# Strided attention: another order of the first loads, and keys and values prepared piecemeal

## The chip, the cores and the metric

The kernel runs on one core of a Trainium2 chip. The metric is device time in microseconds, the median of several executions. The core has five engines that work side by side, each through its own list of instructions in order: TensorE (matrix products; PE in the profile, its weight loads PEld), VectorE (DVE), ScalarE (ACT), GpSimd (POOL) and SyncE (SP). Sixteen DMA engines move data between the chip's main memory (HBM) and the on-chip memory. Here all transfers are issued by SyncE, on one queue.

## What is computed

For each of 8 x 12 = 96 heads, 1024 queries of 64 numbers attend to only 16 keys and values: those at the positions 0, 64, 128 and so on. All is float32 on the outside.

```python
batch, heads, seq, dim = (8, 12, 1024, 64)      # stride = 64
scale = 1.0 / np.sqrt(dim)
for i in range(seq):
    attend_positions = np.arange(0, seq, stride)
    q = Q[:, :, i:i + 1, :].copy()
    k = K[:, :, attend_positions, :].copy()
    v = V[:, :, attend_positions, :].copy()
    scores = np.einsum('bhqd,bhkd->bhqk', q, k) * scale
    weights = np.exp(scores - np.max(scores, axis=-1, keepdims=True))
    weights = weights / (np.sum(weights, axis=-1, keepdims=True) + 1e-10)
    result[:, :, i, :] = np.einsum('bhqk,bhkd->bhqd', weights, v)[:, :, 0, :]
```

Q and the result are 25.2 MB each. Of K and V only a sixteenth is read, 0.39 MB each, in rows of 256 bytes that lie 16 KB apart.

## The kernel before

The heads are worked off in 24 groups of four (`HG`, `NG`). A group's Q block is 1 MB and so is its part of the result. `load(g)` (line 94) brings a Q block as 32 rows of 32 KB into one of 11 buffers (`QBUFS`), `store(g)` (line 250) writes a result block from one of 9 (`OBUFS`). Both go through `_copy`, so line 34 is the issue of every such transfer. K and V are loaded by lines 89 and 90.

The order of all work is written out by hand (`manual_schedule`); each engine executes its instructions in the order of the program.

**Start-up.** SyncE issues K, V and then the first 11 Q blocks. GpSimd makes an identity matrix and from it the two orders of rows and columns `perm_k` and `perm_v` (lines 113 and 120), and casts K twice side by side into `k_dup` (line 116) and V into `v_bf` (line 124), both in bfloat16. VectorE clears `k_t` and the three weight buffers `w` (lines 127, 131) and makes a selector of head slots, `s_sel` and `mask` (lines 138 to 151). Then, for all 24 groups at once, TensorE transposes the keys (line 160), ScalarE copies them into `k_t` (line 166), TensorE sorts the values (line 175), and VectorE multiplies them by the mask, four times for each of four matmul results (line 180), which makes the block-diagonal values `v_bd`.

**A group** goes through four functions:

- `transposes(g, x)`, x = 0 and 1: eight TensorE transposes (line 193) take half a Q block, of which they read the upper 16 bits of each float32 number as bfloat16; a ScalarE copy (line 198) brings the result from the accumulators' memory (PSUM) into `qt`, which has two buffers.
- `scores(g)`: four matmuls of `k_t` with `qt` (line 206), then two exponentials on ScalarE (line 218) into the weight buffer `w`.
- `sums(g)`: eight small matmuls of `w` with `s_sel` (line 227), and a reciprocal on VectorE (line 231).
- `outputs(g, c)`, c = 0 to 3: two matmuls of `w` with `v_bd` (line 238), and one VectorE multiplication by the reciprocals (line 243) into the result block.

Ahead of the loop stand the transposes of groups 0 and 1 and the scores of group 0. An iteration of the loop then is: sums of g, outputs 0 and 1, scores of g+1, output 2, the first transposes of g+2, output 3, the second transposes of g+2, the store of g, and the load of g+11.

Of the kernel before, what the change touches and what calls it, by code (L numbers as in the profile page):

```python
# [11 lines left out]
FP32 = mybir.dt.float32  # L12
BF16 = mybir.dt.bfloat16
I16 = mybir.dt.int16
AF = mybir.ActivationFunctionType
ALU = mybir.AluOpType


def _ap_with(ap: bass.AP, new_ap, extra_offset: int = 0) -> bass.AP:
    return dataclasses.replace(  # L20
        ap, ap=[list(p) for p in new_ap], offset=ap.offset + extra_offset
    )
# [26 lines left out]
def kernel(  # L49
# [8 lines left out]
    nc = tc.nc  # L58

    B, H, S, D = Q.shape  # L60
# [3 lines left out]
    P = 128  # L64
    HG = 4
    NG = B * H // HG
    NC = NG // 2
    SD = S * D
    assert B * H == NG * HG and S == 1024 and D == 64 and NK == 16
    QBUFS = 11  # L70
    OBUFS = 9

    const = ctx.enter_context(tc.tile_pool(name="const", bufs=1))
    qn_pool = ctx.enter_context(tc.tile_pool(name="qn", bufs=QBUFS))
    out_pool = ctx.enter_context(tc.tile_pool(name="outsb", bufs=OBUFS))
    qt_pool = ctx.enter_context(tc.tile_pool(name="qt", bufs=2))
    rec_pool = ctx.enter_context(tc.tile_pool(name="rec", bufs=2))
    psum_qt = ctx.enter_context(tc.tile_pool(name="pqt", bufs=2, space=bass.MemoryType.PSUM))
    psum_sc = ctx.enter_context(tc.tile_pool(name="psc", bufs=2, space=bass.MemoryType.PSUM))
# [6 lines left out]
    k_raw = const.tile([P, NC, D], FP32, name="k_raw")  # L86
    v_raw = const.tile([P, NC, D], FP32, name="v_raw")
    kv_src = [[stride * D, P], [2 * HG * SD, NC], [1, D]]
    nc.sync.dma_start(k_raw, _ap_with(K, kv_src))
    nc.sync.dma_start(v_raw, _ap_with(V, kv_src))  # L90

    qn = {}

    def load(g):
        qn[g] = qn_pool.tile([P, 32 * D], FP32, name="qn", tag="qn")
        _copy(
            nc, qn[g], _ap_with(Q, [[HG * SD // 32, 32], [1, HG * SD // 32]], g * HG * SD)
        )

    for g in range(QBUFS):  # L100
        load(g)


# [4 lines left out]
    perm_k = const.tile([P, 2, 2, 2, NK], BF16, name="perm_k")  # L108

    perm_v = const.tile([P, 2, 2, 2, 2, NK], BF16, name="perm_v")  # L110
    for c in range(2):
        for a in range(2):
            nc.gpsimd.tensor_copy(out=perm_k[:, c, a], in_=id_v[:, c, :, a])
    k_dup = const.tile([P, NC, 2, D], BF16, name="k_dup")
    for e in range(2):
        nc.gpsimd.tensor_copy(out=k_dup[:, :, e], in_=k_raw)  # L116
    for c in range(2):
        for a in range(2):
            for e in range(2):
                nc.gpsimd.tensor_copy(  # L120
                    out=perm_v[:, c, a, :, e], in_=id_v[:, c, :, a]
                )
    v_bf = const.tile([P, NC, D], BF16, name="v_bf")
    nc.gpsimd.tensor_copy(out=v_bf, in_=v_raw)  # L124

    k_t = const.tile([P, NC, 2, 4, 2, NK], BF16, name="k_t")
    nc.vector.memset(k_t, 0.0)  # L127
# [1 line left out]
    for i in range(3):  # L129
        w = const.tile([P, 8, P], BF16, name=f"w{i}")  # L130
        nc.vector.memset(w, 0.0)
        w_bufs.append(w)


    iota_p = const.tile([P, 1], I16, name="iota_p")
    nc.gpsimd.iota(iota_p, pattern=[[0, 1]], base=0, channel_multiplier=1)  # L136
    slot_i = const.tile([P, 1], I16, name="slot_i")
    nc.vector.tensor_scalar(  # L138
        out=slot_i, in0=iota_p, scalar1=4, scalar2=3,
# [1 line left out]
    )  # L141
    slot_f = const.tile([P, 1], FP32, name="slot_f")
    nc.vector.tensor_copy(out=slot_f, in_=slot_i)
    col4 = const.tile([P, 4], I16, name="col4")
    nc.gpsimd.iota(col4, pattern=[[1, 4]], base=0, channel_multiplier=0)
    s_sel = const.tile([P, 4], BF16, name="s_sel")
    nc.vector.tensor_scalar(
        out=s_sel, in0=col4, scalar1=slot_f, scalar2=None, op0=ALU.is_equal
    )
    mask = const.tile([P, 4], FP32, name="mask")  # L150
    nc.vector.tensor_scalar(
        out=mask, in0=col4, scalar1=slot_f, scalar2=None, op0=ALU.is_equal
    )


    pk = perm_k.rearrange("p c a b k -> p (c a b k)")
    for n in range(NC // 4):
        kp = psum_o.tile([P, 4, 2, 4, NK], FP32, name="kp", tag="o")
        for i in range(4):
            nc.tensor.matmul(  # L160
                kp[:, i], lhsT=k_dup[:, 4 * n + i].rearrange("p e d -> p (e d)"),
                rhs=pk, start=True, stop=True,
            )
        for e in range(2):
            h = slice(64 * e, 64 * e + 64)
            nc.scalar.copy(  # L166
                k_t[h, 4 * n : 4 * n + 4, :, :, e].rearrange("p n c s k -> p (n c s) k"),
                kp[h].rearrange("p n c s k -> p (n c s) k"),
            )

    v_bd = const.tile([P, NC, 2, 4, D], BF16, name="v_bd")
    for n in range(2):
        for c in range(2):
            vp = psum_sc.tile([P, NC // 2, D], FP32, name="vp", tag="sc")
            nc.tensor.matmul(  # L175
                vp, lhsT=perm_v[:, c].rearrange("p a b e k -> p (a b e k)"),
                rhs=v_bf[:, 6 * n : 6 * n + 6], start=True, stop=True,
            )
            for s in range(4):
                nc.vector.tensor_scalar(  # L180
                    out=v_bd[:, 6 * n : 6 * n + 6, c, s], in0=vp,
                    scalar1=mask[:, s : s + 1], scalar2=None, op0=ALU.mult,
                )

    qt, wt, rec, out_sb = {}, {}, {}, {}

    def transposes(g, x):
        if x == 0:
            qt[g] = qt_pool.tile([P, 2, 8, P], BF16, name="qt", tag="qt")
        ps = psum_qt.tile([P, 8, P], BF16, name="qt_ps", tag="qt_ps")  # L190
        qb = qn[g].bitcast(BF16)
        for i in range(8):
            nc.tensor.transpose(  # L193
                ps[:, i],
                _ap_with(qb, [qb.ap[0], [2, P]], extra_offset=(8 * x + i) * 2 * P + 1),
                identity,
            )
        nc.scalar.copy(qt[g][:, x], ps)  # L198

    def scores(g):  # L200
        sc = psum_sc.tile([P, 512], FP32, name="sc", tag="sc")
        q = qt[g]
        kt = k_t[:, g // 2, g % 2].rearrange("p s e k -> p (s e k)")
        for j in range(4):
            a, b = divmod(j, 2)
            nc.tensor.matmul(  # L206
                sc[32 * j : 32 * j + 32],
                lhsT=kt[:, 32 * j : 32 * j + 32],
                rhs=_ap_with(
                    q, [q.ap[0], [P, 8], [8 * P, 2], [1, 32]],  # L210
                    extra_offset=32 * (2 * b + a),
                ),
                start=True, stop=True, tile_position=(0, 32 * j),
            )
        w = wt[g] = w_bufs[g % 3]
        for a in range(2):
            wa = w[64 * a : 64 * a + 64]
            nc.scalar.activation(  # L218
                out=_ap_with(wa, [wa.ap[0], [P, 8], [1, 2], [2, 32]], extra_offset=64 * a),
                in_=sc[64 * a : 64 * a + 64].rearrange("p (t x q) -> p t x q", t=8, x=2),  # L220
                func=AF.Exp, bias=0.0, scale=scale,
            )

    def sums(g):
        sm = psum_s.tile([P, 2, 8, 2], FP32, name="sm", tag="sm")
        for i in range(8):
            nc.tensor.matmul(  # L227
                sm[:, :, i], lhsT=wt[g][:, i], rhs=s_sel, start=True, stop=True
            )
        rec[g] = rec_pool.tile([P, 2, 16], FP32, name="rec", tag="rec")  # L230
        nc.vector.reciprocal(rec[g], sm.rearrange("p b i e -> p b (i e)"))  # L231

    def outputs(g, c):
        if c == 0:
            out_sb[g] = out_pool.tile([P, 2, 16, D], FP32, name="out_sb", tag="out_sb")
        ps = psum_o.tile([P, 2, 2, 2 * D], FP32, name="o_ps", tag="o")
        for i in range(2):
            nc.tensor.matmul(  # L238
                ps[:, :, i], lhsT=wt[g][:, 2 * c + i],
                rhs=v_bd[:, g // 2, g % 2].rearrange("p s d -> p (s d)"),  # L240
                start=True, stop=True,
            )
        nc.vector.tensor_tensor(  # L243
            out=out_sb[g][:, :, 4 * c : 4 * c + 4],
            in0=ps.rearrange("p b i (e d) -> p b (i e) d", e=2),
            in1=rec[g][:, :, 4 * c : 4 * c + 4].unsqueeze(3).to_broadcast([P, 2, 4, D]),
            op=ALU.mult,
        )

    def store(g):  # L250
        o = out_sb[g]
        _copy(
            nc,
            _ap_with(out, [[16 * D, P], [2 * SD, 2], [1, 16 * D]], g * HG * SD),
            _ap_with(o, [o.ap[0], [1, 1], [1, 32 * D]]),
        )

    for g in range(2):
        for x in range(2):
            transposes(g, x)  # L260
    scores(0)
    for g in range(NG):
        sums(g)
        outputs(g, 0)
        outputs(g, 1)
        if g + 1 < NG:
            scores(g + 1)
        outputs(g, 2)
        if g + 2 < NG:
            transposes(g + 2, 0)  # L270
        outputs(g, 3)
        if g + 2 < NG:
            transposes(g + 2, 1)
        store(g)
        if g + QBUFS < NG:
            load(g + QBUFS)
# [35 lines left out]
```

The softmax here doesn't subtract the row's maximum and nothing guards it: scores larger than these inputs give would overflow.

## Time and profile before

| What | Value | Where it is from |
|---|---|---|
| median of five executions | 130.43 us (130.31 to 130.78) | the times |
| the profiled execution | 130.44 us | the times |
| its span, first to last instruction | 128.6 us | the page |
| busy: PE, PEld, DVE, ACT, POOL | 69.5, 51.3, 83.8, 86.2, 5.1 us | the page |
| moved by DMA | 51.26 MB, mean 399 GB/s | the page |
| one result multiplication, line 243 | 689 ns, 96 times | groups of the page |
| one copy of transposes, line 198 | 1015 ns, 48 times | groups of the page |
| one exponential, line 218 | 736 ns, 48 times | groups of the page |
| one masking of values, line 180 | 609 ns, 16 times | groups of the page |
| one key copy, line 166 | 580 ns, 6 times | groups of the page |
| one cast of K for all groups, line 116 | 829 ns, twice | groups of the page |
| load of a Q block, issue to landing | 18.9 us, median of 24 | DMA issues of the page |
| store of a result block, issue to landing | 19.5 us, median of 24 | DMA issues of the page |

The span counts from the first to the last instruction; the execution's own time has 1.84 us more around it. The page names busy time by engine, a row of forty slices that says how many of the sixteen DMA engines were busy in each, the DMA queues, the chain of work that ended last, and the costliest groups of instructions. Behind the page stand finer views of the same execution: instructions in order of time, waits by who ended them, and sums over chosen stretches. A transfer's time from issue to landing holds its wait in the queue.

### The profile page before, as it was taken

The numbers are of one execution on the slowest core, as the hardware profiler recorded it, in microseconds if no ns is written. First come the engines' busy times: TensorE is split into PE (matmuls) and PEld (weight loads), VectorE is DVE, ScalarE is ACT, GpSimd is POOL, SyncE is SP. The second block draws the span as 40 slices with busy tenths as digits, with TensorE's granted clock in tenths as the row PEclk, the third lists the DMA queues.
The fourth block names the chain that finished last, engine by engine and source line by source line (L and its number), as shares of the span: only waits on it lengthen the run. The fifth ranks groups of instructions, "written<-read, shape, count | busy, mean of one in ns | idle before, by whom it ended". The sixth has DMA issues, their size and how long they took to land.

```text
span 128.6 us, 2215 instructions
## 1 busy us (share of the span) xinstructions
PE 69.5 (54%) x880; PEld 51.3 (40%) x880; DVE 83.8 (65%) x144; ACT 86.2 (67%) x103; POOL 5.1 (4%) x23
## 2 busy tenths in 40 slices
PE   0071665985656866667766668666677666500000
PEld 0040542764445654445544456544455444300000
DVE  6229963788678777787777787777877777740000
ACT  2173294988889888899888898888998888400000
POOL 4470000000000000000000000000000000000000
PEclk9999997799999999999999999999999999955555
DMA  2998989999799899999999999999998999999970
GB/s 62 346 438 377 469 347 489 408 403 469 321 428 489 357 426 446 405 441 436 398 451 433 392 449 441 392 466 428 395 482 349 426 423 426 418 431 421 426 326 18
DMA packets 7722, 51.26 MB, mean 399 GB/s; under 512 B 3872, under 2 KB 3872, under 8 KB 3872
## 3 DMA queue, kind: packets, MB, share of 16 engines
q1 hardware_dynamic: 7712, 51.12, 96.3%
q8 instruction: 7, 0.11, 0.4%
q14 instruction: 3, 0.02, 0.0%
HBM read 25.95 MB, written 25.17 MB: 398 GB/s over the span
## 4 chain that ended last, share of the span: by engine, by line
ACT 59%; PE 14%; DVE 5%; DMA 3%; POOL 3%; issue 3%; ACTq 1%; DVEq 0%; POOLq 0%
ACT qt L198 33%; ACT w L218 26%; PE sc L206 8%; DVE v_bd L180 3%; DMA k_raw<-in_K_dram 3%; PE qt_ps L193 3%; PE o_ps L238 2%; DVE out_sb L243 1%; POOL k_dup L116 1%; POOL perm_v L120 1%; PE sm L227 1%; POOL v_bf L124 1%; ACTq L307 1%; DVEq L307 0%; PE vp L175 0%
## 5 line engine op out<-in xcount | busy, mean ns | idle before, releaser
L243 DVE TENSOR_TENSOR out_sb<-o_ps,rec 128x512 f32<-128x512 f32 x96 | 63.3, 689 | 15.2 <-PE o_ps L238 12.9
L198 ACT COPY qt<-qt_ps 128x1024 bf16<-128x1024 bf16 x48 | 46.2, 1015 | 5.2 <-PE qt_ps L193 4.7
L218 ACT ACTIVATE w<-sc 64x512 bf16<-64x512 f32 x48 | 35.3, 736 | 13.2 <-PE sc L206 12.9
L238 PE MATMUL o_ps<-v_bd,w 128*128 128x256 bf16 x192 | 33.5, 279 | 0.6 <-DVE out_sb L243 0.6
L193 PE MATMUL qt_ps<-identity,qn 128*128 128x128 bf16 x384 | 30.9, 227 | 0.2 <-ACT qt L198 0.2
L193 PEld LDWEIGHTS <-qn 128*128 128x128 bf16 x384 | 27.1, 103 | 3.9 <-issue 2.6
L206 PE MATMUL sc<-qt,k_t 128*32 128x512 bf16 x96 | 9.8, 396 | 24.4 <-ACT qt L198 24.4
L238 PEld LDWEIGHTS <-w 128*128 128x128 bf16 x192 | 14.3, 98 | 6.9 <-issue 6.2
L206 PEld LDWEIGHTS <-k_t 128*32 128x32 bf16 x96 | 4.4, 93 | 29.2 <-issue 29.1
L231 DVE RECIPROCAL rec<-sm 128x32 f32<-128x32 f32 x24 | 8.6, 358 | 8.9 <-PE sm L227 8.9
L227 PE MATMUL sm<-s_sel,w 128*128 128x4 bf16 x192 | 8.5, 166 | 6.8 <-ACT w L218 4.8
L227 PEld LDWEIGHTS <-w 128*128 128x128 bf16 x192 | 6.4, 96 | 10.9 <-ACT w L218 10.9
L180 DVE TENSOR_SCALAR v_bd<-vp,mask 128x384 bf16<-128x384 f32 x16 | 8.5, 609 | 0.1
L166 ACT CAST k_t<-kp 64x512 bf16<-64x512 f32 x6 | 3.5, 580 | 3.5 <-PE kp L160 3.4
L160 PE MATMUL kp<-perm_k,k_dup 128*128 128x128 bf16 x12 | 1.5, 309 | 6.6 <-POOL k_dup L116 6.6
L175 PE MATMUL vp<-v_bf,perm_v 128*128 128x384 bf16 x4 | 1.8, 490 | 4.6 <-DVE v_bd L180 4.1
L160 PEld LDWEIGHTS <-k_dup 128*128 128x128 bf16 x12 | 1.2, 141 | 6.6 <-POOL k_dup L116 6.6
L138 DVE TENSOR_SCALAR slot_i<-iota_p 128x1 int16<-128x1 int16 x1 | 0.2, 156 | 4.6 <-POOL iota_p L136 4.6
L166 ACT ACT_TABLE_LOAD x1 | 1.3, 1283 | 2.5 <-DVE k_t L127 2.5
L127 DVE MEMSET k_t<- 128x1536 uint32 x1 | 1.3, 1338 | 1.1 <-PEq L293 1.1
L175 PEld LDWEIGHTS <-perm_v 128*128 128x128 bf16 x4 | 0.5, 126 | 3.7 <-issue 3.7
L116 POOL CAST k_dup<-k_raw 128x768 bf16<-128x768 f32 x2 | 1.6, 829 | 2.9 <-DMA k_raw<-in_K_dram 2.9
(15 smaller groups left out, 6.0 us busy)
## 6 DMA issues: line engine op xcount, KB each, us to landing
qn<-in_Q_dram SPq DMA_DIRECT2D x24, 1024.0 KB, 18.9
out_dram<-out_sb SPq DMA_DIRECT2D x24, 1024.0 KB, 19.5
k_raw<-in_K_dram SPq DMA_DIRECT2D x1, 384.0 KB, 4.2
v_raw<-in_V_dram SPq DMA_DIRECT2D x1, 384.0 KB, 5.4
```

Source lines behind the costliest of these rows:

```text
L116: nc.gpsimd.tensor_copy(out=k_dup[:, :, e], in_=k_raw)
L160: nc.tensor.matmul(kp[:, i], lhsT=k_dup[:, 4 * n + i].rearrange("p e d -> p (e d)"), rhs=pk, start=True, stop=True,)
L166: nc.scalar.copy(k_t[h, 4 * n : 4 * n + 4, :, :, e].rearrange("p n c s k -> p (n c s) k"), kp[h].rearrange("p n c s k -> p (n c s) k"),)
L180: nc.vector.tensor_scalar(out=v_bd[:, 6 * n : 6 * n + 6, c, s], in0=vp, scalar1=mask[:, s : s + 1], scalar2=None, op0=ALU.mult,)
L193: nc.tensor.transpose(ps[:, i], _ap_with(qb, [qb.ap[0], [2, P]], extra_offset=(8 * x + i) * 2 * P + 1), identity,)
L198: nc.scalar.copy(qt[g][:, x], ps)
L206: nc.tensor.matmul(sc[32 * j : 32 * j + 32], lhsT=kt[:, 32 * j : 32 * j + 32], rhs=_ap_with(q, [q.ap[0], [P, 8], [8 * P, 2], [1, 32]], ext ...
L218: nc.scalar.activation(out=_ap_with(wa, [wa.ap[0], [P, 8], [1, 2], [2, 32]], extra_offset=64 * a), in_=sc[64 * a : 64 * a + 64].rearrange( ...
L227: nc.tensor.matmul(sm[:, :, i], lhsT=wt[g][:, i], rhs=s_sel, start=True, stop=True)
L231: nc.vector.reciprocal(rec[g], sm.rearrange("p b i e -> p b (i e)"))
L238: nc.tensor.matmul(ps[:, :, i], lhsT=wt[g][:, 2 * c + i], rhs=v_bd[:, g // 2, g % 2].rearrange("p s d -> p (s d)"), start=True, stop=True,)
L243: nc.vector.tensor_tensor(out=out_sb[g][:, :, 4 * c : 4 * c + 4], in0=ps.rearrange("p b i (e d) -> p b (i e) d", e=2), in1=rec[g][:, :, 4 ...
```

## The change

- Q block 0 is loaded first, then K and V, then Q blocks 1 to 10. Later loads and stores keep their order.
- Keys are prepared in three parts of eight groups. `keys(n)` casts a third of K on VectorE instead of GpSimd, transposes it and copies it. The first part stands ahead of the loop, the others at the end of iterations 1 and 3.
- V is cast on VectorE. The sorted values are copied unmasked into `v_rep` by `value_rows()`, in four copies; `values(g)` then multiplies them by a mask for one group at a time on GpSimd, into one of three buffers `vb`, two groups ahead in the loop. `outputs` reads `vb[g]` instead of `v_bd`.
- The mask is now 128 x 4 x 64 bfloat16 numbers, and the two small index tables are made earlier.
- The start-up order is: transposes of group 0, first keys, scores of group 0, values, transposes of group 1. An iteration is: values and the first transposes of g+2, sums of g, output 0, scores of g+1, output 1, second transposes of g+2, outputs 2 and 3, in iterations 1 and 3 a third of the keys, the store of g, the load of g+11.

```diff
+    vb_pool = ctx.enter_context(tc.tile_pool(name="vb", bufs=3))
...
-    nc.sync.dma_start(k_raw, _ap_with(K, kv_src))
-    nc.sync.dma_start(v_raw, _ap_with(V, kv_src))
...
-    for g in range(QBUFS):
+    load(0)
+    nc.sync.dma_start(k_raw, _ap_with(K, kv_src))
+    nc.sync.dma_start(v_raw, _ap_with(V, kv_src))
+    for g in range(1, QBUFS):
         load(g)
...
-    k_dup = const.tile([P, NC, 2, D], BF16, name="k_dup")
-    for e in range(2):
-        nc.gpsimd.tensor_copy(out=k_dup[:, :, e], in_=k_raw)
...
-    v_bf = const.tile([P, NC, D], BF16, name="v_bf")
-    nc.gpsimd.tensor_copy(out=v_bf, in_=v_raw)
...
-    mask = const.tile([P, 4], FP32, name="mask")
-    nc.vector.tensor_scalar(
-        out=mask, in0=col4, scalar1=slot_f, scalar2=None, op0=ALU.is_equal
-    )
...
+    mask = const.tile([P, 4, D], BF16, name="mask")
+    nc.vector.tensor_copy(out=mask, in_=s_sel.unsqueeze(2).to_broadcast([P, 4, D]))
...
+    def keys(n):
+        for e in range(2):
+            nc.vector.tensor_copy(
+                out=k_dup[:, 4 * n : 4 * n + 4, e], in_=k_raw[:, 4 * n : 4 * n + 4]
+            )
         kp = psum_o.tile([P, 4, 2, 4, NK], FP32, name="kp", tag="o")
...
-            for s in range(4):
-                nc.vector.tensor_scalar(
-                    out=v_bd[:, 6 * n : 6 * n + 6, c, s], in0=vp,
-                    scalar1=mask[:, s : s + 1], scalar2=None, op0=ALU.mult,
...
+    def value_rows():
+        nc.vector.tensor_copy(out=v_bf, in_=v_raw)
+        for n in range(2):
+            for c in range(2):
+                vp = psum_sc.tile([P, NC // 2, D], FP32, name="vp", tag="sc")
+                nc.tensor.matmul(
+                    vp, lhsT=perm_v[:, c].rearrange("p a b e k -> p (a b e k)"),
+                    rhs=v_bf[:, 6 * n : 6 * n + 6], start=True, stop=True,
                 )
+                nc.vector.tensor_copy(out=v_rep[:, 6 * n : 6 * n + 6, c], in_=vp)
...
+    def values(g):
+        vb[g] = vb_pool.tile([P, 4, D], BF16, name="vb", tag="vb")
+        nc.gpsimd.tensor_tensor(
+            out=vb[g], in0=mask,
+            in1=v_rep[:, g // 2, g % 2].unsqueeze(1).to_broadcast([P, 4, D]),
+            op=ALU.mult,
+        )
...
-                rhs=v_bd[:, g // 2, g % 2].rearrange("p s d -> p (s d)"),
+                rhs=vb[g].rearrange("p s d -> p (s d)"),
...
-    for g in range(2):
-        for x in range(2):
-            transposes(g, x)
+    transposes(0, 0)
+    transposes(0, 1)
+    keys(0)
     scores(0)
+    value_rows()
+    values(0)
+    values(1)
+    transposes(1, 0)
+    transposes(1, 1)
     for g in range(NG):
+        if g + 2 < NG:
+            values(g + 2)
+            transposes(g + 2, 0)
         sums(g)
         outputs(g, 0)
-        outputs(g, 1)
         if g + 1 < NG:
             scores(g + 1)
-        outputs(g, 2)
-        if g + 2 < NG:
-            transposes(g + 2, 0)
-        outputs(g, 3)
+        outputs(g, 1)
         if g + 2 < NG:
             transposes(g + 2, 1)
+        outputs(g, 2)
+        outputs(g, 3)
+        if g in (1, 3):
+            keys((g + 1) // 2)
         store(g)
```

## The prediction

> **What bounds the kernel now.** The page comes first: the span, the DMA row, the queues, and the chain that ended last.
>
> ```profile
> span 128.6 us, 2215 instructions
> ...
> DMA  2998989999799899999999999999998999999970
> ...
> q1 hardware_dynamic: 7712, 51.12, 96.3%
> q8 instruction: 7, 0.11, 0.4%
> ...
> ACT 59%; PE 14%; DVE 5%; DMA 3%; POOL 3%; issue 3%; ACTq 1%; DVEq 0%; POOLq 0%
> ```
>
> Two readings compete. The chain is 59% ScalarE, so it looks as if the transpose copies (L198) and exponentials (L218) set the time. The queue row says that packets of SyncE's own queue fill 96.3% of what 16 DMA engines have in the whole span. What decides is the end: who waits for whom on SyncE, and when it issues.
>
> ```profile
> SPq L307 <- DMA out_dram<-out_sb: 12.8, 1, 12.8
> ```
>
> ```profile
> 0.74 0.44 SPq L89 DMA_DIRECT2D k_raw<-in_K_dram  x1
> 1.23 0.71 SPq L90 DMA_DIRECT2D v_raw<-in_V_dram  x1
> 1.99 12.61 SPq L34 DMA_DIRECT2D qn<-in_Q_dram  x11
> 25.15 0.63 SPq L34 DMA_DIRECT2D out_dram<-out_sb  x1
> ...
> 60.08 0.47 SPq L34 DMA_DIRECT2D qn<-in_Q_dram  x1
> ...
> 64.98 0.47 SPq L34 DMA_DIRECT2D qn<-in_Q_dram  x1
> ...
> 82.16 32.50 SPq L34 DMA_DIRECT2D out_dram<-out_sb  x11
> ```
>
> The last store is issued at 82.16 + 32.50 = 114.7 us, when all arithmetic is over, and SyncE then waits 12.8 us for stores already in the queue. One group moves one load and one store and takes 64.98 - 60.08 = 4.90 us there, while the ScalarE part of the chain repeats every 3.94 us (its exponentials start at 38.43 and 42.37). So compute runs ahead and stands in line behind the DMA engines. The chain view doesn't see this, since it follows the instructions and not the packets. Only three things can move the end: bytes, time in which DMA engines stand idle, and the rate of packets. The stretches with DMA engines below 1.00 are at the two ends (columns: stretch, length, busy time of PE, PEld, DVE, ACT, POOL, clock, share of 16 DMA engines, GB/s; a share over 1 means small packets that overlap in one engine):
>
> ```profile
> 0.00:1.83 1.83, 0.00 (x0) 0.00 (x0) 0.70 (x1) 0.00 (x0) 1.17 (x10) 1.00 0.00 0
> 1.83:2.23 0.40, 0.00 (x0) 0.00 (x0) 0.40 (x1) 0.00 (x0) 0.20 (x2) 1.00 0.29 74
> 2.23:2.63 0.40, 0.00 (x0) 0.00 (x0) 0.34 (x2) 0.08 (x1) 0.00 (x0) 1.00 0.20 51
> 2.63:3.03 0.40, 0.00 (x0) 0.00 (x0) 0.37 (x1) 0.40 (x1) 0.00 (x0) 1.00 1.03 236
> 3.03:4.03 1.00, 0.00 (x0) 0.00 (x0) 0.92 (x2) 0.80 (x1) 0.00 (x0) 1.00 1.28 289
> 4.03:5.45 1.42, 0.00 (x0) 0.00 (x0) 0.06 (x1) 0.00 (x0) 0.48 (x1) 1.00 1.35 222
> ...
> 16.00:26.00 10.00, 6.77 (x70) 4.73 (x68) 5.90 (x11) 7.86 (x10) 0.00 (x0) 0.83 1.00 419
> ...
> 125.00:126.00 1.00, 0.00 (x0) 0.00 (x0) 0.00 (x0) 0.00 (x0) 0.00 (x0) 0.50 0.24 98
> 126.00:127.20 1.20, 0.00 (x0) 0.00 (x0) 0.00 (x0) 0.00 (x0) 0.00 (x0) 0.50 0.05 20
> ```
>
> From 6 us to 122 us the share is 0.97 to 1.02 in every ten-microsecond stretch, so nothing stands idle in the middle. The queue starts 1.1 us after the first issue (0.74 to 1.83) and then trickles for 0.8 us: the first 256-byte packets of K keep 0.29 and 0.20 of the engines busy. At the end 0.05 of 16 engines is one engine, which works alone. It presumably is the one that also carries TensorE's program: the instruction queue moves 7 pieces, about one per 256 instructions.
>
> **Compute: many edits, one answer.** Removed from VectorE are 16 multiplies of 609 ns (L180, 8.5 us, 9.6 to 18.1 us) and from GpSimd the two casts of K (829 ns each) and the one of V (830 ns). VectorE gets six part casts of K, one of V, four copies from PSUM and the wider mask. GpSimd gets 24 multiplies of 128x256. No row has such a multiply. Its cost lies between the 211 ns copy of 128x32 and twice the 830 ns cast of 128x768, which holds three times the elements on one input, so 0.2 to 1.7 us. I take 0.6 us, nearer to the cast of equal output size scaled down and doubled for two inputs. ScalarE's six key copies (580 ns) and TensorE's matmuls keep their number; four key copies and eight key matmuls move into groups 1 and 3.
>
> In the start-up Q block 0 lands about 5 us (before: 1.99 + 7.2 = 9.2), but K and V one block later, 2.5 us at 419 GB/s, less what is saved below: K near 6.5 (before 0.74 + 4.2 = 4.9), V near 8.3 (before 1.23 + 5.4 = 6.6). Two transposes, the first keys and scores fill the wait for V; behind V's cast on TensorE stand the value matmuls and, behind those, the transposes of group 1. In the loop TensorE now waits for Q block g+2 before the sums of g: `transposes(g + 2, 0)` holds sums, outputs, and with them VectorE and the store behind it. While only loads flow, a block comes each 2.5 us, faster than a group is worked off. Block 2 lands near 13 and the first store can go out at 17 to 19 us (before 25.15).
>
> All of it costs nothing at the end, because a cover hides it: the eleven first loads and K and V are 12.3 MB, 29 us at 419 GB/s, so the DMA engines need no store before 33 us or so. Either kernel's first store is there over 7 us sooner. Per group the cover is 4.90 - 3.94 = 0.96 us; the two groups with extra keys add 2 x 0.58 us of ScalarE once each, against a lead of 12.8 us at the end. If that cover were gone each group would cost what it is over 4.90 us, 24 times. The earlier stores gain nothing either: they stand later in the same queue order.
>
> The Trainium skill speaks against the GpSimd part: "GPSIMD Engine Reference", section "Elementwise — side-by-side cycle accounting", has two-input work there at 1.96 times VectorE's time and keeps VectorE as the rule for elementwise work. By its 4497 ns for 2048 elements, a multiply of 256 would be estimated at 0.56 us and 24 of them at 13.5 us, more than the 8.5 us taken off VectorE; a sum over engines would call it a loss. No row here shows the multiply.
>
> **DMA order: the one edit on the path.** SyncE issues the same 50 transfers, with Q block 0 ahead of K and V; bytes and packets are the same. Each engine now begins with large packets, while K's and V's small ones are made ready behind them. What falls away is the trickle: 0.40 x (1 - 0.29) + 0.40 x (1 - 0.20) = 0.28 + 0.32 = 0.60 us of idle DMA engines. By another way: K and V are 393 KB each; K at 289 GB/s takes 1.36 us, V at 222 GB/s 1.77 us, together 3.13 us, while Q's first packets began about 5.7, so 3.87 us after 1.83: 0.74 us. Bounds: if both go at V's rate beside later issues, 786 / 222 = 3.54 us, gain 0.33; both at K's, 786 / 289 = 2.72 us, gain 1.15. If the trickle belongs to K's own packets and is paid again, 0. I take 0.60, the smaller of the two workings.
>
> **The tail** keeps its term: same stores, same 7 program pieces (TensorE's instructions don't change in number, 1760), 0. An eighth piece would need some 250 more instructions.
>
> Sum: span 128.6 - 0.6 = 128.0 us. The profiled execution took 130.44 us, 1.84 around its span, and the median is 130.43, so the two agree and the forecast is **129.8 us**.
>
> **Rivals.**
> (A) The forecast, 129.3 to 130.1 us: chance 0.62.
> (B) The trickle is paid again, by K behind Q, or hidden nowhere: the bound is the same and the time 130.4 us. For it: the trickle might come from K's rows lying 16 KB apart, not from an empty start. Against: a packet took no longer then; there were only few of them. Chance 0.18.
> (C) Slower: a gap after V. In the first trace the third issue took 2.08 us (the longest of the Q loads) and ended at 4.07, while V's packets flowed until 5.45; it was held by the small transfers ahead. If Q block 1 is held until V has drained, the engines stand empty for a whole issue-to-packet delay, 1.83 - 0.74 = 1.09 us: 130.43 + 1.09 - 0.60 = 130.9, or 131.5 if the trickle comes back too; 131.2 between. For it: block 1 is now the load behind them. Against: the issue came free 1.4 us before V's end, more than the 1.09 needed. It decides from a gap of 0.60 us up, and shows as slower from 0.99. Chance 0.14.
> The Trainium skill's "DMA: Bandwidth & Descriptors", section "Specifications", gives that first delay as some 0.6 us, and by it C would end at 130.4, no loss; the trace's 1.09 decides.
> (D) Compute becomes the bound: a group over 4.90 us, by a GpSimd multiply near 5 us or the hold of sums behind Q block g+2; at 5.2 us each, 24 x 0.3 = 7.2 us, 137.6 us. Against: 0.2 to 1.7 us by the rows. Chance 0.03.
> (E) The chain view is right after all: then the start 6 to 8 us earlier shows in full, near 123.5 us. Against: 12.8 us of waiting for stores. Chance 0.03.
>
> **Numbers.** A measurement of this kernel can't tell less than about 0.3%, 0.39 us, from no change. Of A 0.54 is beyond that, with E 0.57 faster; A's rest 0.08 and B's 0.16 make 0.24 the same; C 0.14, D 0.03 and 0.02 of B make 0.19 slower. The range 129.2 to 131.0 us holds nearly all of A and B and the milder end of C, about 8 in 10; A alone is 129.3 to 130.1.
>
> **What would show it.** The share of DMA engines in 0.4 us stretches from 1.83 us: near 1 from the start (A), low again behind Q block 0 (B), or a hole between V and block 1 (C). The first store's issue near 18 us and a longer wait of SyncE at the end, beyond 15 us, with the end itself almost unmoved: that is the cover. The group's distance on SyncE should stay at 4.9 us and the stretch after 125 us should again have one engine. I am wrong if the middle falls below 0.95, or if SyncE's last wait is short.

## The result, and the profile after

The changed kernel takes 131.13 us in the median of 20 executions (130.44 to 131.33), the kernel before 130.37 us in 39; the ratio of their means is 1.0048, 95% interval 1.0039 to 1.0056. By this ratio it became slower by 0.6 us (the medians lie 0.76 us apart), where 0.6 us less was forecast. The profiled execution took 130.79 us, 0.35 us more than the one before.

The page of the changed kernel:

```profile
span 129.0 us, 2250 instructions
...
DMA  5799798997999999999999999999998999999980
...
q1 hardware_dynamic: 7712, 51.12, 96.8%
q8 instruction: 7, 0.11, 0.4%
...
DVE 1%; DVEq 0%; issue 0%
...
L187 POOL TENSOR_TENSOR vb<-mask,v_rep 128x256 bf16<-128x256 bf16 x24 | 16.0, 668 | 80.8 <-PE o_ps L246 69.0
```

The chain that ended last was 59% ScalarE and is now 1% VectorE. The time hardly moved, so ScalarE's share of that chain had never bounded it: the chain follows instructions, and what ends last here are packets. Their queue fills 96.8% of the span, the packets and bytes are those of before, and so are the seven pieces of program. Next, SyncE's waits (us in total, times, longest) and what it issues (start, length):

```profile
SPq L323 <- DMA out_dram<-out_sb: 16.9, 2, 14.7
```

```profile
0.73 0.58 SPq L34 DMA_DIRECT2D qn<-in_Q_dram  x1
1.37 0.56 SPq L99 DMA_DIRECT2D k_raw<-in_K_dram  x1
1.97 0.93 SPq L100 DMA_DIRECT2D v_raw<-in_V_dram  x1
2.95 12.09 SPq L34 DMA_DIRECT2D qn<-in_Q_dram  x10
19.90 0.63 SPq L34 DMA_DIRECT2D out_dram<-out_sb  x1
...
61.00 0.47 SPq L34 DMA_DIRECT2D qn<-in_Q_dram  x1
...
65.91 0.47 SPq L34 DMA_DIRECT2D qn<-in_Q_dram  x1
...
83.09 28.01 SPq L34 DMA_DIRECT2D out_dram<-out_sb  x11
```

The first store goes out at 19.90 instead of 25.15 us, and the last at 111.1 instead of 114.7, while the end came later. The pace of a group is again 65.91 - 61.00 = 4.91 us. TensorE has become so early that it waits for Q blocks, 18.8 us in all:

```profile
PE qt_ps L201 <- DMA qn<-in_Q_dram: 18.8, 9, 6.1
```

So much of the lead that compute won was spent in waiting. The sums over stretches of the start, in the columns of the prediction:

```profile
1.83:2.23 0.40, 0.00 (x0) 0.00 (x0) 0.40 (x1) 0.18 (x1) 0.40 (x5) 1.00 2.56 655
2.23:2.63 0.40, 0.00 (x0) 0.00 (x0) 0.34 (x2) 0.00 (x0) 0.40 (x4) 1.00 0.76 246
2.63:3.03 0.40, 0.00 (x0) 0.00 (x0) 0.37 (x1) 0.00 (x0) 0.40 (x4) 1.00 1.14 410
3.03:4.03 1.00, 0.00 (x0) 0.00 (x0) 0.92 (x3) 0.00 (x0) 0.34 (x3) 1.00 0.08 33
4.03:5.45 1.42, 0.00 (x0) 0.00 (x0) 0.74 (x5) 0.00 (x0) 0.00 (x0) 1.00 0.86 351
```

A packet counts whole in the stretch in which it starts. All that started before 5.45 us is 655 x 0.4 + 246 x 0.4 + 410 x 0.4 + 33 + 351 x 1.42 = 1056 KB: block 0 with its 1049 KB, and hardly anything else. The first eight packets of 32 KB start by 2.23 us and the next ones up to 3.03, and the second of each engine starts only near 4 us and later. A block that goes at 2.48 us once the queue runs has taken until about 5.5.

No view prints when each engine ends its part of a transfer, but the trace holds it: every engine closes a transfer with a write of 4 bytes (800 of them: 50 transfers, 16 engines). The mean of the 16 (us), in the order of issue in each kernel:

| Kernel | 1st | 2nd | 3rd | 4th |
|---|---|---|---|---|
| before | K 3.89 | V 5.63 | Q0 8.38 | Q1 10.86 |
| changed | Q0 5.48 | K 6.91 | V 8.71 | Q1 11.45 |

From there on both go in steps of 2.48 us a block while only loads flow. Q1 is 0.59 us late, which is about the loss. The block behind V takes 0.27 us longer than that in both (2.75 for Q0 before, 2.74 for Q1 after), and V 1.74 and 1.80 us. What differs is the first place, counted from the first issue: K takes 3.15 us there and 1.43 behind a Q block, so its start costs 1.72; Q0 takes 4.75 there, against a pace of 2.48, so its start costs 2.27. 2.27 - 1.72 = 0.55 us, and V's 0.06: that makes Q1's 0.59 but for rounding.

### The profile page after: what moved, and what is told of

The parts are those of the page before. It is cut to its first block, busy times and chain, and to the rows that moved or that the text cites. A ratio compares the mean times of both kernels' runs of the same rounds, so it can differ in the third digit from the quotient of the medians.

```text
span 129.0 us, 2250 instructions
## 1 busy us (share of the span) xinstructions
PE 73.6 (57%) x880; PEld 51.8 (40%) x880; DVE 77.8 (60%) x139; ACT 85.2 (66%) x103; POOL 18.7 (14%) x44
## 3 DMA queue, kind: packets, MB, share of 16 engines
q1 hardware_dynamic: 7712, 51.12, 96.8%
## 5 line engine op out<-in xcount | busy, mean ns | idle before, releaser
L251 DVE TENSOR_TENSOR out_sb<-o_ps,rec 128x512 f32<-128x512 f32 x96 | 62.3, 687 | 8.0 <-PE o_ps L246 5.6
L206 ACT COPY qt<-qt_ps 128x1024 bf16<-128x1024 bf16 x48 | 47.3, 1014 | 18.5 <-PE qt_ps L201 17.9
L201 PE MATMUL qt_ps<-identity,qn 128*128 128x128 bf16 x384 | 33.4, 239 | 19.1 <-DMA qn<-in_Q_dram 18.8
L201 PEld LDWEIGHTS <-qn 128*128 128x128 bf16 x384 | 28.3, 108 | 23.9 <-DMA qn<-in_Q_dram 21.5
L246 PE MATMUL o_ps<-vb,w 128*128 128x256 bf16 x192 | 35.3, 290 | 0.7 <-DVE out_sb L251 0.7
L187 POOL TENSOR_TENSOR vb<-mask,v_rep 128x256 bf16<-128x256 bf16 x24 | 16.0, 668 | 80.8 <-PE o_ps L246 69.0
L246 PEld LDWEIGHTS <-w 128*128 128x128 bf16 x192 | 14.9, 101 | 7.7 <-issue 6.7
L214 PE MATMUL sc<-qt,k_t 128*32 128x512 bf16 x96 | 10.5, 424 | 6.5 <-ACT qt L206 5.3
L235 PEld LDWEIGHTS <-w 128*128 128x128 bf16 x192 | 7.1, 98 | 7.3 <-ACT w L226 7.1
L214 PEld LDWEIGHTS <-k_t 128*32 128x32 bf16 x96 | 3.6, 94 | 12.0 <-issue 10.5
L182 DVE CAST v_rep<-vp 128x384 bf16<-128x384 f32 x4 | 2.2, 558 | 1.9 <-PE vp L178 1.8
L156 DVE CAST k_dup<-k_raw 128x256 bf16<-128x256 f32 x6 | 1.5, 286 | 2.9 <-DMA k_raw<-in_K_dram 2.9
L132 DVE MEMSET w<- 128x512 uint32 x3 | 1.5, 485 | 0.2
```

The lines of the kernel that those rows point to most:

```text
L182: nc.vector.tensor_copy(out=v_rep[:, 6 * n : 6 * n + 6, c], in_=vp)
L187: nc.gpsimd.tensor_tensor(out=vb[g], in0=mask, in1=v_rep[:, g // 2, g % 2].unsqueeze(1).to_broadcast([P, 4, D]), op=ALU.mult,)
L201: nc.tensor.transpose(ps[:, i], _ap_with(qb, [qb.ap[0], [2, P]], extra_offset=(8 * x + i) * 2 * P + 1), identity,)
L214: nc.tensor.matmul(sc[32 * j : 32 * j + 32], lhsT=kt[:, 32 * j : 32 * j + 32], rhs=_ap_with(q, [q.ap[0], [P, 8], [8 * P, 2], [1, 32]], ext ...
L235: nc.tensor.matmul(sm[:, :, i], lhsT=wt[g][:, i], rhs=s_sel, start=True, stop=True)
L246: nc.tensor.matmul(ps[:, :, i], lhsT=wt[g][:, 2 * c + i], rhs=vb[g].rearrange("p s d -> p (s d)"), start=True, stop=True,)
```

## The experiments

Each ran beside the kernel before, on the same chip. In the expectations, theory S puts the loss into these first transfers, and a rival C (not the prediction's, which is a gap after V) into the compute edits.

**The order of loads alone.** In the kernel before:

```diff
-    nc.sync.dma_start(k_raw, ...)
-    nc.sync.dma_start(v_raw, ...)
-    for g in range(QBUFS):
+    load(0)
+    nc.sync.dma_start(k_raw, ...)
+    nc.sync.dma_start(v_raw, ...)
+    for g in range(1, QBUFS):
         load(g)
```

> The kernel before with one edit: Q block 0 issued ahead of K and V; all compute as before. Theory S (the loss is made in the first 9 us of the DMA queue: the engines come up slowly whoever is first, and large packets that start then lose more; the refill after small packets, first Q packet 1.49 instead of 1.22 us, is paid for block 0 and again for block 1): the second Q block lands about 0.45 us later than in the kernel before, and the time is 130.8 to 131.1 us, ratio 1.003 to 1.006. Rival C (the compute edits cost it: GpSimd's multiplies, another pace of TensorE, another moment of program fetches): 130.4 us, ratio 0.999 to 1.001.

Measured: 131.05 us, ratio 1.0052 (1.0039 to 1.0065). Means of the engines: Q0 5.51, K 6.94, V 8.74, Q1 11.52, so Q1 is 0.66 us late. The stretches of the start:

```profile
0.70:1.90 1.20, 0.00 (x0) 0.00 (x0) 0.78 (x1) 0.00 (x0) 1.03 (x6) 1.00 0.00 0
1.90:2.30 0.40, 0.00 (x0) 0.00 (x0) 0.40 (x1) 0.00 (x0) 0.12 (x1) 1.00 2.57 655
2.30:2.70 0.40, 0.00 (x0) 0.00 (x0) 0.34 (x2) 0.15 (x1) 0.00 (x0) 1.00 0.00 0
2.70:3.10 0.40, 0.00 (x0) 0.00 (x0) 0.34 (x2) 0.40 (x1) 0.00 (x0) 1.00 1.67 655
```

655 GB/s x 0.4 us is 262 KB, eight packets of 32 KB: half of the engines start just after 1.9 us, the other half only after 2.70, 2 us behind the issue. The first half gained nothing by it: its packets took 2.57 x 16 x 0.40 / 8 = 2.06 us each and those of the second half 1.67 x 16 x 0.40 / 8 = 1.34, where 16 engines at 419 GB/s need 1.25, so that both halves end their first packet between 4.1 and 4.4 us. This one edit makes the whole loss, without any change in compute.

**The compute edits alone.** In the changed kernel:

```diff
-    load(0)
     nc.sync.dma_start(k_raw, ...)
     nc.sync.dma_start(v_raw, ...)
-    for g in range(1, QBUFS):
+    for g in range(QBUFS):
         load(g)
```

> The changed kernel with one part undone: K and V issued first again, then Q blocks 0 to 10; all compute edits stay. Theory S: 130.4 us, ratio 0.999 to 1.001, second Q block landed where the kernel before has it, the last store issued some 3 us sooner without effect. Rival C: 130.8 to 131.1 us. If both this and the order alone are slower, each by about half, the loss has two parts.

Measured: 130.58 us against 130.46, ratio 1.0015 (1.0005 to 1.0025); Q1 at 10.84, where the kernel before has it. It ran a second time, beside the two relatives that follow:

> The changed kernel with K and V first again, a second time, as the measure for the two kernels beside it: 1.0005 to 1.0025 as the first time if the rest is real, within 0.001 of 1 if it was spread.

Measured: 130.55 us against 130.44, ratio 1.0010 (0.9997 to 1.0022). The first relative has the multiplies on VectorE:

```diff
     def values(g):
-        nc.gpsimd.tensor_tensor(
+        nc.vector.tensor_tensor(
```

> The changed kernel with K and V first again, and with the 24 multiplies of values on VectorE instead of GpSimd. With K and V first the compute edits were left with 0.15% (0.05 to 0.25). Their traces show a fourth 8 KB piece of program fetched, where the kernel before has three. If that piece is GpSimd's longer program and costs the rest, there are three here and the ratio is 1.000 within 0.001. If the rest comes from the loop's order or is no more than spread, the ratio stays near 1.0015.

Measured: 130.56 us, ratio 1.0008 (0.9991 to 1.0024), and still four 8 KB pieces of program, so the fourth isn't GpSimd's longer program. On VectorE the multiply took 282 ns, on GpSimd 668. The last relative is the kernel before with the order of the loop alone:

```diff
     for g in range(NG):
+        if g + 2 < NG:
+            transposes(g + 2, 0)
         sums(g)
...
```

> The kernel before with the changed order inside the loop alone (transposes of g+2 ahead of the sums of g, scores after output 0); loads, keys, values and start-up as before. The DMA queue has the same transfers in the same order, so 130.4 us, ratio 1.000 within 0.001, with the last store issued sooner. If TensorE's other pace costs the rest of 0.15% seen with K and V first, 1.001 to 1.002.

Measured: 130.30 us, ratio 0.9989 (0.9978 to 1.0001), with the last store issued 4 us sooner. What the compute edits cost lies between nothing and 0.25%; these runs can't place it, and it isn't needed for the loss.

**The size of the first packets.** In the changed kernel, block 0 as 128 rows of 8 KB:

> The changed kernel, but block 0 alone is read as 128 rows of 8 KB in place of 32 rows of 32 KB (same bytes, same place). If theory S holds because large packets are caught in the slow start, 8 KB packets lose less: 130.7 to 130.9 us, 0.2 to 0.4 us under the changed kernel. If the start is a fixed delay plus the refill at each turn from small to large packets, no difference: 131.0 to 131.2 us. Under C no difference either.

Measured: 131.00 us, ratio 1.0048 (1.0034 to 1.0062). Q0 ends at 5.51 and Q1 at 11.47, as with 32 KB. So the loss doesn't hang on the packet's size: either way the engines are up to their pace some 2.3 us after the issue (5.51 - 0.73 - 2.48).

**Block 0 between K and V**, in the kernel before. The "turn" is the passage from 256-byte packets to large ones in the queue:

> The kernel before with Q block 0 issued between K and V. K is still first in the queue, so nothing large meets the slow start, but the turn from small to large packets comes twice. If that turn is the cost: 0.27 us more, 130.6 to 130.7 us, ratio 1.002. If only a large first transfer costs: 130.4 us, ratio 1.000 within 0.001. Under C 130.4 us too.

Measured: 130.69 us, ratio 1.0013 (1.0002 to 1.0025), which by itself would fit a second turn. The trace speaks against it. Means: K 4.05, Q0 6.61, V 8.09, Q1 10.83. Two turns cost less than expected: the block behind V takes 2.74 us as ever, the one behind K 2.56, 0.08 over its pace; and V away from K takes 1.49 instead of 1.74, so Q1 is where it was. The turn is no part of the loss: both kernels of the study have one behind V. The rest of 0.13% isn't in the first transfers. In the profiled executions the median of the 16 engines lands the last store 0.16 us later than in the kernel before, and the engine that lands last comes 2.45 us after that median, before 2.21; the cause stays open.

**A twelfth of K first, then block 0:**

```diff
-    nc.sync.dma_start(k_raw, ...)
+    nc.sync.dma_start(k_raw[:, 0:1], ...)
+    load(0)
+    nc.sync.dma_start(k_raw[:, 1:12], ...)
     nc.sync.dma_start(v_raw, ...)
...
```

> The kernel before with a twelfth of K (128 packets of 256 bytes) issued first, then Q block 0, the rest of K, V, the other Q blocks. Two parts of the 0.6 us are told apart: that a large first transfer starts some 0.25 us later than a small one, and that the turn from small to large packets is paid for block 0 and again for block 1. If the late start is part of it, the tiny transfer takes it away: second Q block 0.2 to 0.3 us sooner than with Q block 0 first, time 130.7 to 130.8 us. If the engines come up slowly by the clock whoever is first, the tiny transfer changes nothing: 131.0 to 131.1 us.

Measured: 131.34 us, ratio 1.0073 (1.0061 to 1.0085): worse than either theory had it. The small piece is through at 1.99 us, block 0's first packets start from 2.53 to 3.56, and Q0 ends at 5.99, Q1 at 11.81. Block 0 was issued at 1.18 and took 4.81 us from there, as in the first place (4.75). So it isn't a matter of the first issue or of engines that have done nothing yet: what is late is a transfer's work after its own issue, and with an almost empty queue nothing covers that.

**Block 0 first by the other kind of call**, the one that K and V use, in the kernel with the order alone:

```diff
-    load(0)
+    qn[0] = qn_pool.tile([P, 32 * D], FP32, name="qn", tag="qn")
+    nc.sync.dma_start(qn[0], _ap_with(Q, [[HG * SD // P, P], [1, HG * SD // P]]))
```

> The kernel before with Q block 0 first, as in the order alone, but loaded by the same kind of call as K and V, in 128 rows of 8 KB. In the runs so far the engines of a first Q transfer come up 1.36 to 2.2 us after its issue begins, those of K 1.1 to 1.9 us. If that comes from the way the Q loads are written, the first block lands 0.3 us sooner and the time is 130.7 to 130.8 us. If it belongs to any first transfer of a Q block, and the rest of the loss to the block behind V (2.75 instead of 2.48 us), it is 131.0 to 131.1 us as with the order alone.

Measured: 130.85 us, ratio 1.0037 (1.0025 to 1.0050). Its issue on SyncE, and its first stretch:

```profile
0.73 0.40 SPq L98 DMA_DIRECT2D qn<-in_Q_dram  x1
```

```profile
0.70:1.90 1.20, 0.00 (x0) 0.00 (x0) 0.77 (x1) 0.00 (x0) 1.03 (x6) 1.00 0.49 55
```

The issue takes 0.40 us where the other kind took 0.58, and the first packets start before 1.90 us, where the order alone had none. Q0 ends at 5.19 and Q1 at 11.22, 0.30 us sooner than with the order alone; the three traces with the block first by the old call have Q1 at 11.45 to 11.52. The 8 KB rows can't be what helped, as the experiment on the size of the packets shows. So by Q1 nearly half of the loss is the form of that first call. The times, 1.0037 against 1.0052, have intervals that overlap and don't settle the share. The start of a Q block still costs 5.19 - 0.73 - 2.48 = 1.98 us against K's 1.72.

**K and V behind six Q blocks**, to measure the cover:

> The kernel before with K and V issued behind Q blocks 0 to 5. It measures the cover. V lands some 15 us later than before, near 22 us, and the first store follows it by 18.5 us as before (25.15 - 6.65), near 40.5 us, while the first loads run out near 33 us. If the cover ends there, the DMA engines stand empty some 7 to 9 us and the time is 138 to 140 us. If compute hardly matters (or can catch up otherwise), only the 0.6 us of the order shows: 131 us.

Measured: 140.9 us, ratio 1.0805 (1.0789 to 1.0821). Its first store and its stretches:

```profile
40.55 0.63 SPq L34 DMA_DIRECT2D out_dram<-out_sb  x1
```

```profile
34.00:38.00 4.00, 2.07 (x21) 0.85 (x18) 1.30 (x3) 2.10 (x3) 0.00 (x0) 1.00 0.00 0
38.00:42.00 4.00, 3.97 (x36) 3.05 (x36) 2.75 (x6) 3.49 (x4) 0.00 (x0) 1.00 0.10 37
```

The loads run out before 34 us as worked out, the engines stand at 0.00, and the time grows by 10.5 us, 0.9 us beyond the expected range. The cover of compute is real and ends where the sum put it; the change stayed well inside it.

**K and V on ScalarE's queue:**

```diff
-    nc.sync.dma_start(k_raw, ...)
-    nc.sync.dma_start(v_raw, ...)
+    nc.scalar.dma_start(k_raw, ...)
+    nc.scalar.dma_start(v_raw, ...)
```

> The kernel before with K and V issued by ScalarE on its own queue, beside the Q blocks of SyncE's. No turn from small to large packets in one queue and no empty engine while small packets are made ready. If the slow start and the turns are what the order of one queue costs: K and V land later (near 8 to 16 us), the time is 130.0 to 130.4 us, at best 0.4 us under the kernel before. If the slow start is paid by whoever is first, Q blocks now: 130.6 to 131.0 us. If the small packets are held too long between the large ones, the first store comes after 33 us and the time grows by what it is late.

Measured: 140.55 us, ratio 1.0776 (1.0755 to 1.0798). The issues, with us to landing:

```profile
k_raw<-in_K_dram ACTq DMA_DIRECT2D x1, 384.0 KB, 19.4
v_raw<-in_V_dram ACTq DMA_DIRECT2D x1, 384.0 KB, 20.5
```

Before 4 us 930 of the 3072 small packets start. Then the Q blocks come, and beside each large packet hardly more than one small one passes: from 4 to 18 us 270 of them start, 19 a us, beside 13 a us of 32 KB. The rest got through between 18 and 21 us, when no packet of a Q block moved, and by then the cover was gone: the first store went out at 40.4 us. The same with Q blocks 0 to 3 in 8 KB packets, and its control on one queue:

> K and V on ScalarE's queue beside the Q blocks, as in the run that lost its cover, but Q blocks 0 to 3 in 128 rows of 8 KB. There, from 10 to 18 us, both queues together moved 460 GB/s against 420, and K and V took 17 us since few small packets passed between two 32 KB ones. If the small packets then cost an engine little, and pass sooner between 8 KB packets, K and V land near 8 to 11 us, the first store is issued before 30 us, and the 3.1 us that K and V take alone in one queue shrink: 128.0 to 129.5 us. If K and V take their 3.1 us of the engines in any queue, and the late start is paid too: 130.5 to 131.2 us. If they still land after 15 us, the cover is short again: over 133 us.

> The kernel before with Q blocks 0 to 3 in 8 KB rows and nothing else, the measure for the kernel beside it. The packets of stores have this size and rate, so 130.4 us, ratio 1.000 within 0.001; if the turn after V is a matter of the large packet's size, up to 0.2 us less.

Measured: 140.21 us, ratio 1.0753 (1.0722 to 1.0784), K and V landed at 20.4 and 21.8 us; the control 130.42 us, ratio 1.0003 (0.9995 to 1.0012). Beside 8 KB packets more small ones pass (47 a us beside 39), but K and V still land after 20 us, so in these runs a second queue saved nothing of their 3.1 us. Whether it could, if the cover held, they can't tell. The 460 GB/s were no safe sign of it: over the whole of 4 to 18 us the first of the two runs moved 431. In the control the block behind V took 2.74 us as ever, so the turn isn't a matter of the large packets' size.

**The last store in 120 and 8 partitions**, in the kernel before (in outline):

```diff
-        _copy(nc, <all 128 partitions>)
+        for lo, hi in ((0, 120), (120, P)) if g == NG - 1 else ((0, P),):
+            _copy(nc, <partitions lo to hi>)
```

> The kernel before with its last store cut into 120 and 8 rows of partitions, so that the first part goes to 15 engines and the second to 8. In all profiles so far one engine lands 2 to 3 us after the median of the 16 at the end. If that engine is the one that the first part leaves out, the end comes 1 to 2 us sooner: 128.6 to 129.6 us. If it is another, its share grows by a fifteenth: 130.4 to 130.7 us.

Measured: 131.11 us, ratio 1.0059 (1.0041 to 1.0077), more than either way it was expected to go. The stretches of its end:

```profile
126.00:127.00 1.00, 0.00 (x0) 0.00 (x0) 0.00 (x0) 0.00 (x0) 0.00 (x0) 0.50 0.14 57
127.00:128.00 1.00, 0.00 (x0) 0.00 (x0) 0.00 (x0) 0.00 (x0) 0.00 (x0) 0.50 0.06 25
```

0.14 of 16 engines is more than two, where the kernel before had 0.05 after 126 us, less than one: to leave an engine out of the first part didn't take the late one away. Which engine it is, and why the loss is so large, stays open.

## Why the prediction was wrong

**Right:** what bounds the kernel. Compute moved by 3.6 us (the last store's issue) to 5.3 us (the first's) and the end didn't follow. The pace stayed at 4.91 us, the last wait grew to 14.7 us (beyond 15 was forecast), the first store came at 19.90 where 17 to 19 was worked out, GpSimd's multiply took 668 ns where 0.6 us was taken. The estimate of 0.56 us from the Trainium skill's "GPSIMD Engine Reference", section "Elementwise — side-by-side cycle accounting", was near that row. The page's rule to keep such work on VectorE made no difference to the time here (1.0008 with it, 1.0010 without), since the 24 multiplies lie under the cover. The size of the cover, 33 us, was confirmed by taking it away.

**Wrong:** the price of the first transfer's start, in the one step on the path: "Each engine now begins with large packets, while K's and V's small ones are made ready behind them. What falls away is the trickle". It took the trickle for a property of small packets and let anything else run at its pace 1.09 us after the issue. For K the start was read rightly: 1.09 + 0.60 of trickle = 1.69, against 1.72 by the engines' means. For Q0 it was forecast as 1.09 and measured 2.27, 1.18 us more. The traces show it in the order alone: the second eight engines start after 2.70 us, the packets of the first eight take 2.06 us in place of 1.25, while K was up to pace by 2.63. That one term makes the difference between -0.60 and the measured +0.6 (-0.60 + 1.18 = 0.58). The rest of the sum was as forecast: K behind Q0 1.43 us (1.36), V 1.80 (1.77). The prediction's rival B named the mechanism, a start that is paid again, but at K's price and so as no change; that it could be dearer for a Q block wasn't considered, though no row showed a Q block as first transfer and the wait should have been bounded from both sides. The runs settle that the start costs this, and by the traces the form of the call is 0.3 us of it; what in the making of a transfer takes so long they don't show.

Theory S had a second part, a turn from small to large packets that is paid twice, and this fell too: block 0 in the first place pays its start and no turn, and the turn behind V is in both kernels.

The prediction's rival C, the gap after V, saw a real hold, at the wrong price: block 1's issue lasted 3.99 us in the order alone and in the changed kernel, longer than the 2.08 before, but ended near 6.95 us, 1.8 us before V, and no hole followed. Rivals D and E are out: the pace of a group stayed, and ScalarE's share of the chain fell from 59% to nothing without a gain in time. None of the kernels tried beats the one before beyond its interval; the order of the loop alone is nearest (0.9989).

## What to carry to other kernels

Where the DMA engines are full from end to end, sum the queue and not the engines' chain: an edit is worth what it does to the first transfer's start and to the last landing; work that lies under the queue's lead moves nothing, until the lead is used up, and then every microsecond counts. The idle stretch ahead of the first transfer isn't won by putting a larger one there; put first what comes up fastest, and measure a transfer in the first place rather than price it there by its pace in the stream. Check by one run which of two parts of a change lies on that path; here it was the place of one issue.

## What the runs showed of the hardware

- A first transfer works on all 16 engines some 1.9 us (K) or 2.0 to 2.3 us (a Q block) after its issue begins; its first packets come after 1.1 us (K) and 1.36 us (a Q block by `_copy`). Packets of a Q block that start sooner than the others take longer (2.06 against 1.34 us in the order alone) and end with them. The Trainium skill's "DMA: Bandwidth & Descriptors", section "Specifications", has about 0.6 us to the first byte; the traces here show 1.0 us or more to the first packet in every run.
- A Q block directly behind V's small packets takes 2.74 to 2.83 us instead of 2.48, behind K's 2.56.
- 256-byte packets of V directly behind K's took 1.72 to 1.81 us, behind a Q block 1.49 us, for the same bytes. The cause wasn't looked for.
- Between two queues an engine passed some 1.5 packets of 256 bytes for each of 32 KB (19 against 13 a us), and 1.2 for each of mostly 8 KB (47 against 39). The same page, in "Queues, rings and completion order", lets an engine drain a packet of some 9 to 17 descriptors from one queue before it switches; the length of a turn no run here shows.
- One engine lands the last store 1.9 to 2.5 us after the median of the 16 in the traces of before, the changed kernel, the order alone and block 0 between K and V. Its lateness jumps by 1.1 to 1.5 us soon after the first piece of the instruction queue q8 is fetched (22.6 to 30.1 us), and rises again from near 100 us, to 2.2 to 2.7 us; that the pieces cause it is an inference from the times.
